# Fetching the token-major x one granule earlier, its squares ahead of the fifth granule's cast, and 1/rms and one normalisation one granule up

## The chip, the cores and the metric

The kernel runs on one NeuronCore of one Trainium2 chip. The metric is the device time of one execution in microseconds, the median of the runs; lower is better. All inputs are in HBM as fp32 when the time starts, and the fp32 result lies in HBM when it ends. The core has a matrix engine (TensorE, PE in the rows; its weight loads are PEld), a vector engine (VectorE, DVE), a scalar engine (ScalarE, ACT), GpSimd (POOL) and a queue that only issues transfers (SyncE, SP).

## The reference, cut to what matters

One decoder layer on 256 tokens of width 2048. An RMS norm, one wide input projection in nine parts, block attention and a gated spatial unit side by side, two projections merged by sigmoid gates, an output projection and the residual:

```
h = rms_norm(x, norm_g)                 # x * rsqrt(mean(x*x) + 1e-6) * g, per token
q, k, v, z_a, u_b, v_b, z_b, g_a, g_b = split(h @ w_in)
q, k = rms_norm per head
y_a = (attention(q, k, v) * silu(z_a)) @ w_proj_a
y_b = (gelu(u_b) * (W_s norm(gelu(v_b)) + b) * silu(z_b)) @ w_proj_b
out = x + (sigmoid(g_a) * y_a + sigmoid(g_b) * y_b) @ w_out
```

The change concerns the first line alone: when the sum of squares of each token is formed, and when the factor 1/rms made from it is applied to x.

## The kernel before, in words

**Granules.** All weights come in one stream of granules of 1 MB, 128 partitions x 2048 fp32. `schedule()` (L47) lists them: eight for q (numbers 0 to 7), eight for k, then v, z_a, v_b, u_b, z_b, the gates, the two projections and the output. Granule i is loaded by `load` into a tile `raw`, of which there are four, so that granule 4 waits for the release of granule 0's, and so on; from granule 10 on the tiles `t` of the Strassen granules share these four buffers.

**Split fp32.** Every fp32 operand is made into a high part and a low part. `halve` (L119) casts `raw` to `wh` on ScalarE (L120) and subtracts on VectorE to get `wl` (L121). A product then takes three matmuls: low x by `wh`, high x by `wh`, high x by `wl` (`three`, L274). A granule of q is eight such products into four accumulators, 24 matmuls of 128x512.

**q without 1/rms.** q is computed from x times the gain alone (`split_x`, L191: two gain multiplications on ScalarE at L195, the cast `xuh` at L198, the subtraction `xul` on VectorE at L199, for two of the sixteen row tiles of x at a time). The factor 1/rms is a number for each token and is put on when q leaves PSUM (L629). From k on the projections use a normalised x, which must therefore be ready before granule 8.

**The factor 1/rms.** x by tokens, two tiles `xnat` of 128 tokens x 2048 (1 MB each), is loaded at L180. `stats` squares each tile on ScalarE with a running sum (L233) and then calls `rsqrt`: one VectorE instruction (L228) and one power on GpSimd (L229) give `rstd`. `stats_row` (L236) has TensorE transpose `rstd` into a row, broadcast over the partitions (`ps_R`, L239), and ScalarE copies it to SBUF (L240). `normalise(i)` (L245) multiplies half i of x by that row on VectorE (L247). `halves_x` casts and subtracts (`xh`, `xl`, L252 and L253), `forms` and `halves_f` make the sums of x for Strassen's products (`F`, `Fh`, `Fl`).

**Order.** One loop over the granules (L601) issues, at granule i: the load of granule i+3, the split of granule i+2, for i below 4 the split of x for granule i+4, the matmuls of granule i, and then what was registered for i by `at` (L530). So the squares, registered in the kernel before at granule 2, stand on ScalarE's queue behind the cast of granule 4. For ScalarE and VectorE the order of the code is kept up to the end of granule 7 (the block opened at L588 and closed at L603). The order on TensorE and SyncE, and on all engines from granule 8 on, is made by the framework's planner from its own estimates: it can let later work go ahead of an instruction that it believes not yet ready. Each engine carries out its queue strictly in the order that was made.

**The first loads**, on SyncE's queue in the order of L165 to L180: pieces of granule 0 and 1 and of x by features, granule 2, x tiles 8 to 11, granule 3, x tiles 12 to 15, the two `xnat` tiles. Granules 4, 5, ... follow from the loop.

Of the kernel before, what the change touches and what calls it, by code (L numbers as in the profile page):

```python
# [20 lines left out]
P = 128  # L21
S = 256
# [42 lines left out]
def hybrid_layer_kernel(  # L65
# [9 lines left out]
    nc = tc.nc  # L75
# [10 lines left out]
    def slot(dtype, name):  # L86
        return big.tile([P, WORDS], dtype, tag="big", name=name)
# [17 lines left out]
    def load_piece(i, a, b):  # L105
        nc.sync.dma_start(raw[i][:, a:b], w[i, :, a:b])

    def new_raw(i):
        raw[i] = wpool.tile([P, WORDS], F32, tag="raw", bufs=4, name=f"raw{i}")

    def load(i, pieces=1):
        if i >= NG:
            return
        new_raw(i)
        n = WORDS // pieces
        for a in range(pieces):
            load_piece(i, a * n, (a + 1) * n)
# [43 lines left out]
    def load_x(p0, p1):  # L161
        nc.sync.dma_start(xt[p0 // 8][:, p0 % 8:(p1 - 1) % 8 + 1, :],
                          xT[:, NVEC + p0 * S:NVEC + p1 * S].rearrange("p (k t) -> p k t", t=S))
# [9 lines left out]
    load_x(4, 8)  # L173
    load(2, pieces=2)
    load_x(8, 12)
    load(3)
    load_x(12, 16)
    xn = [slot(F32, f"xnat{m}") for m in range(2)]
    for m in range(2):
        nc.sync.dma_start(xn[m], x[m * P:(m + 1) * P, :])  # L180
    for i in range(2):
        xu_h.append(slot(F32R, f"xuh{i}").rearrange("p (k t) -> p k t", t=S))
        xu_l.append(slot(F32R, f"xul{i}").rearrange("p (k t) -> p k t", t=S))
# [346 lines left out]
    def at(i, fn, *a):  # L530
        later.setdefault(i, []).append((fn, a))
# [5 lines left out]
        fn(*a, free["banks"][n0:n1])  # L537

    i0 = first["q", 0]
    at(i0 + 2, stats)  # L540
    at(i0 + 3, stats_row)
    at(i0 + 4, normalise, 1)
    at(i0 + 4, halves_x, 1)
    at(i0 + 5, normalise, 0)
    at(i0 + 5, forms)
# [2 lines left out]
    i0 = first["k", 0]  # L548
    at(i0 + 1, sums, None, "q")
    at(i0 + 3, norm_qk, "q")  # L550
    i0 = first["v", 0]
# [3 lines left out]
    i0 = first["za", 0]  # L555
# [4 lines left out]
    i0 = first["vb", 0]  # L560
# [6 lines left out]
    i0 = first["ub", 0]  # L567
# [4 lines left out]
    i0 = first["zb", 0]  # L572
# [3 lines left out]
    i0 = first["g", 0]  # L576
# [148 lines left out]
```

## Time and profile before

| | |
|---|---|
| median of 3 runs | 687.62 us (687.28 to 688.37) |
| the profiled execution's own time | 687.05 us |
| its span, first to last instruction | 685.3 us |
| busy share of the span: TensorE, VectorE, ScalarE, GpSimd | 97%, 81%, 57%, 5% |
| granted TensorE clock, mean | 0.995 of full speed |
| HBM read, written | 132.72 MB, 2.10 MB |

The span runs from the first to the last instruction; 1.75 us of the execution's time lie outside it. A row of the timeline gives the start in microseconds, the duration, the engine (SPq is SyncE's queue), the source line, the operation, out<-in, shapes and how many were merged (x2), and in brackets how long the engine was idle before it and what released it. A granted clock of 1.00 is TensorE's higher level, 2.4 GHz, and 0.50 the lower, 1.2 GHz.

### The profile page before, as it was taken

How to read it: one execution, taken by the hardware profiler on the slowest of the kernel's cores; microseconds unless marked ns; L12 is line 12 of the kernel's file. 1: busy time of each engine (PE TensorE's matmuls, PEld its weight loads, DVE VectorE, ACT ScalarE, POOL GpSimd, SP SyncE). 2: the span in 40 equal slices, each digit the busy share in tenths (PEclk: the TensorE clock that was granted, in tenths of full speed). 3: DMA queues.
4: the chain of work that ended last, by engine and by line, in shares of the span. 5: the costliest groups of instructions: out<-in, count | busy, mean ns of one | idle time of the engine just before them, and what ended most of it. 6: DMA issues, size and time to landing. Idle time of an engine off the chain costs nothing.

```text
span 685.3 us, 7695 instructions
## 1 busy us (share of the span) xinstructions
PE 664.1 (97%) x3018; PEld 545.4 (80%) x3018; DVE 554.3 (81%) x504; ACT 390.4 (57%) x459; POOL 31.9 (5%) x28
## 2 busy tenths in 40 slices
PE   8789999999999999999989999999999999999997
PEld 5578778778888887788777888888888888888886
DVE  4569989889899899998998998878869886754551
ACT  7678757765775585665745735663554555333330
POOL 1000401200000007000000000000000000000000
PEclk9989999999999999999999999999999999999999
DMA  8952653483373535634735824844664466857610
GB/s 312 418 193 67 241 213 117 166 303 124 119 280 129 229 134 184 245 103 153 297 125 223 304 85 185 315 175 184 230 239 143 188 258 225 261 184 233 235 46 31
DMA packets 21923, 135.31 MB, mean 197 GB/s; under 512 B 2432, under 2 KB 3072, under 8 KB 6656
## 3 DMA queue, kind: packets, MB, share of 16 engines
q1 hardware_dynamic: 20736, 132.73, 52.4%
q10 hardware_dynamic: 1152, 2.10, 1.2%
q8 instruction: 23, 0.38, 0.2%
q14 instruction: 12, 0.10, 0.0%
HBM read 132.72 MB, written 2.10 MB: 197 GB/s over the span
## 4 chain that ended last, share of the span: by engine, by line
PE 69%; DVE 15%; issue 5%; ACT 4%; DMA 4%; SPq 1%; POOL 0%; DVEq 0%; ACTq 0%
PE acc_g L279 14%; PE y L279 13%; PE acc_out L279 13%; PE seven_g L279 5%; PE acc_za L279 4%; PE acc_vb L279 4%; DMA raw<-in_w 4%; DVE wl L121 3%; ACT th L120 2%; PE acc_zb L279 2%; DVE wlp L121 2%; PE acc_v L279 2%; DVE t L138 2%; DVE tl L121 2%; PE acc_ub L279 2%
## 5 line engine op out<-in xcount | busy, mean ns | idle before, releaser
L121 DVE TENSOR_TENSOR wl<-raw,wh 128x2048 fp32r<-128x2048 f32 (+2 forms) x87 | 183.2, 2116 | 68.0 <-ACT wh L120 67.8
L120 ACT CAST wh<-raw 128x2048 fp32r<-128x2048 f32 (+2 forms) x87 | 153.7, 1774 | 103.8 <-PE acc_out L279 45.7
L120 ACT CAST th<-t 128x2048 fp32r<-128x2048 f32 x40 | 76.4, 1911 | 106.9 <-DVE t L141 102.2
L121 DVE TENSOR_TENSOR tl<-t,th 128x2048 fp32r<-128x2048 f32 x40 | 91.6, 2291 | 29.1 <-ACT th L120 28.6
L279 PE MATMUL acc_out<-wh,mT 128*128 128x512 f32 x256 | 79.0, 390 | 0.0
L120 ACT CAST whp<-raw 128x1536 fp32r<-128x1536 f32 x40 | 59.2, 1482 | 29.9 <-DMA raw<-in_w 18.9
L121 DVE TENSOR_TENSOR wlp<-raw,whp 128x1536 fp32r<-128x1536 f32 x40 | 70.5, 1763 | 0.0
L279 PEld LDWEIGHTS acc_out<-wh,mT 128*128 128x128 f32 x256 | 47.9, 188 | 9.8
L279 PE MATMUL acc_out<-wl,mT 128*128 128x512 f32 x128 | 49.8, 389 | 0.0
L279 PE MATMUL acc_g<-wh,xh 128*128 128x512 f32 x128 | 49.8, 389 | 0.0
L279 PE MATMUL acc_g<-wh,xl 128*128 128x512 f32 x128 | 49.7, 389 | 0.0
L138 DVE TENSOR_TENSOR t<-raw 128x1024 f32<-128x1024 f32 x40 | 49.2, 1230 | 0.5
L279 PE MATMUL acc_g<-wl,xh 128*128 128x512 f32 x128 | 48.8, 389 | 0.0
L229 POOL TENSOR_TENSOR rs<-ms,mhalf 128x4 f32<-128x4 f32 x12 | 25.2, 2119 | 128.4 <-DVE ms L228 128.4
L279 PEld LDWEIGHTS acc_g<-wl,xh 128*128 128x128 f32 x128 | 24.0, 188 | 5.1
L279 PEld LDWEIGHTS acc_g<-wh,xl 128*128 128x128 f32 x128 | 24.0, 188 | 5.1
L279 PEld LDWEIGHTS acc_out<-wl,mT 128*128 128x128 f32 x128 | 24.0, 188 | 5.0
L279 PEld LDWEIGHTS acc_g<-wh,xh 128*128 128x128 f32 x128 | 24.0, 188 | 4.9
L140 DVE TENSOR_TENSOR t<-t,raw 128x512 f32<-128x512 f32 x40 | 27.5, 689 | 0.3
L141 DVE TENSOR_TENSOR t<-t,raw 128x512 f32<-128x512 f32 x40 | 27.5, 688 | 0.3
L279 PE MATMUL acc_q<-wh,xuh 128*128 128x512 f32 x64 | 25.5, 399 | 1.6 <-ACT wh L120 1.6
L279 PE MATMUL acc_q<-wl,xuh 128*128 128x512 f32 x64 | 25.7, 401 | 0.3 <-DVE wl L121 0.2
(453 smaller groups left out, 1427.8 us busy)
## 6 DMA issues: line engine op xcount, KB each, us to landing
raw<-in_w SPq DMA_DIRECT2D x117, 1024.0 KB, 4.9
raw<-in_w SPq DMA_DIRECT2D x5, 512.0 KB, 7.3
xnat<-in_x SPq DMA_DIRECT2D x2, 1024.0 KB, 13.3
xres<-in_x ACTq DMA_DIRECT2D x8, 256.0 KB, 5.8
out<-xres SPq DMA_DIRECT2D x7, 256.0 KB, 4.7
xt<-in_xT SPq DMA_DIRECT2D x3, 512.0 KB, 9.9
raw<-in_w SPq DMA_DIRECT2D x2, 256.0 KB, 4.6
ws<-in_wsT SPq DMA_DIRECT2D x2, 256.0 KB, 2.9
```

Source lines behind the costliest of these rows:

```text
L120: nc.scalar.copy(h, r)
L121: nc.vector.tensor_tensor(l, r, f(h), op=ALU.subtract)
L138: nc.vector.tensor_tensor(two, r[:, B:3 * B].rearrange("p (a n) -> p a n", a=2), r[:, None, 0:B].to_broadcast([P, 2, B]), op=ALU.add)
L140: nc.vector.tensor_tensor(t[:, 2 * B:3 * B], t[:, 0:B], r[:, 2 * B:3 * B], op=ALU.add)
L141: nc.vector.tensor_tensor(t[:, 3 * B:], t[:, 2 * B:3 * B], r[:, 3 * B:], op=ALU.add)
L229: nc.gpsimd.tensor_tensor(dst, ms[:, :n], mhalf[:, :n], op=ALU.pow)
L279: nc.tensor.matmul(acc, a, b, start=(start and n == 0), stop=(stop and n == 2))
```

## The change

The loads of the two `xnat` tiles move from behind x tiles 12 to 15 to around the load of granule 3: the first ahead of it, the second behind it, and x tiles 12 to 15 come ahead of both. Three registrations change: `stats` from granule 2 to granule 1, so that the squares stand in front of the cast of granule 4 on ScalarE's queue; `normalise(1)` from granule 4 to granule 3, so that it stands in front of granule 6's subtraction on VectorE's queue. `stats_row` stays at granule 3, `halves_x(1)` at granule 4. (The diff's first registration line moves `stats`; 1/rms is formed inside it.) No instruction is added or left out.

```
     load(2, pieces=2)
     load_x(8, 12)
-    load(3)
     load_x(12, 16)
     xn = [slot(F32, f"xnat{m}") for m in range(2)]
-    for m in range(2):
-        nc.sync.dma_start(xn[m], x[m * P:(m + 1) * P, :])
+    nc.sync.dma_start(xn[0], x[0:P, :])
+    load(3)
+    nc.sync.dma_start(xn[1], x[P:S, :])
...
     i0 = first["q", 0]
-    at(i0 + 2, stats)
+    at(i0 + 1, stats)
     at(i0 + 3, stats_row)
-    at(i0 + 4, normalise, 1)
+    at(i0 + 3, normalise, 1)
     at(i0 + 4, halves_x, 1)
```

## Rows read from the trace of the kernel before

**Rows 1.** Busy time in stretches of the span. The columns: the stretch in us from the span's start and its length; busy us of TensorE, its weight loads, VectorE, ScalarE and GpSimd, each with its number of instructions; the granted TensorE clock, the busy share of the DMA engines, GB/s.

```profile
29.80:36.50 6.70, 0.00 (x0) 0.00 (x0) 3.06 (x3) 6.67 (x9) 0.69 (x1) 0.72 1.01 415
36.50:40.00 3.50, 3.43 (x10) 2.83 (x11) 2.66 (x2) 3.47 (x6) 0.02 (x1) 0.56 0.21 89
...
250.00:685.30 435.30, 426.48 (x1922) 351.88 (x1919) 341.24 (x298) 216.35 (x196) 13.92 (x4) 1.00 0.52 191
```

**Rows 2.** TensorE's timeline: the start of granule 3, its last matmul, the transposes of 1/rms, granule 4's first matmuls, and the start of granule 8 (the first of k).

```profile
24.15 0.39 PE L279 MATMUL acc_q<-wh,xul 128*128 128x512 f32 x1
...
29.36 0.39 PE L279 MATMUL acc_q<-wl,xuh 128*128 128x512 f32 x1
36.57 0.69 PE L239 MATMUL ps_R<-ident,rstd 128*128 128x128 f32 x2 [6.82 <-POOL rstd L229]
36.91 0.78 PE L279 MATMUL acc_q<-wh,xul 128*128 128x512 f32 x1
...
39.19 0.58 PE L279 MATMUL acc_q<-wl,xuh 128*128 128x512 f32 x1
39.60 0.40 PE L279 MATMUL acc_q<-wh,xul 128*128 128x512 f32 x1
...
60.04 0.39 PE L279 MATMUL acc_k<-wh,xl 128*128 128x512 f32 x1
```

**Rows 3.** ScalarE's timeline from the cast of granule 3 to that of granule 6 and `xh`.

```profile
19.41 1.91 ACT L120 CAST wh<-raw 128x2048 fp32r<-128x2048 f32 x1
...
28.36 1.91 ACT L120 CAST wh<-raw 128x2048 fp32r<-128x2048 f32 x1 [5.58 <-DMA raw<-in_w]
30.17 0.91 ACT L195 ACTIVATE xt<-xt,xv 128x256 f32<-128x256 f32 x2
...
31.63 1.91 ACT L233 ACTIVATE xnat<-xnat 128x2048 f32<-128x2048 f32 x1
...
35.43 1.88 ACT L120 CAST wh<-raw 128x2048 fp32r<-128x2048 f32 x1
...
38.67 0.37 ACT L240 COPY xv<-ps_R 128x256 f32<-128x256 f32 x1
38.94 1.91 ACT L120 CAST wh<-raw 128x2048 fp32r<-128x2048 f32 x1
45.41 1.91 ACT L252 CAST xh<-xt 128x2048 fp32r<-128x2048 f32 x1 [4.56 <-DVE xt L247]
```

**Rows 4.** VectorE's timeline from granule 3's subtraction to the second normalisation, and granule 8's subtraction; then GpSimd's row for the power.

```profile
21.36 2.29 DVE L121 TENSOR_TENSOR wl<-raw,wh 128x2048 fp32r<-128x2048 f32 x1 [1.17 <-ACT wh L120]
...
30.30 2.29 DVE L121 TENSOR_TENSOR wl<-raw,wh 128x2048 fp32r<-128x2048 f32 x1 [6.05 <-ACT wh L120]
...
37.34 2.29 DVE L121 TENSOR_TENSOR wl<-raw,wh 128x2048 fp32r<-128x2048 f32 x1 [1.62 <-ACT wh L120]
...
40.88 2.29 DVE L121 TENSOR_TENSOR wl<-raw,wh 128x2048 fp32r<-128x2048 f32 x1 [0.65 <-ACT wh L120]
43.09 2.29 DVE L247 TENSOR_TENSOR xt<-xt,xv 128x2048 f32<-128x2048 f32 x1
47.35 2.29 DVE L253 TENSOR_TENSOR xl<-xt,xh 128x2048 fp32r<-128x2048 f32 x1 [1.98 <-ACT xh L252]
...
51.77 2.28 DVE L247 TENSOR_TENSOR xt<-xt,xv 128x2048 f32<-128x2048 f32 x1
...
58.17 2.28 DVE L121 TENSOR_TENSOR wl<-raw,wh 128x2048 fp32r<-128x2048 f32 x1
...
35.81 0.71 POOL L229 TENSOR_TENSOR rstd<-ms,mhalf 128x2 f32<-128x2 f32 x1 [32.71 <-DVE ms L228]
```

**Rows 5.** Transfers: SyncE's issues (start, duration) of granule 3, x tiles 12 to 15 and granule 4, and, from the view of the transfers issued in that moment, KB and us from issue to landing of granule 3, x tiles 12 to 15 and granule 4; last the lines of the view of `xnat` with the issues of its two tiles and their times to landing.

```profile
8.48 0.33 SPq L106 DMA_DIRECT2D raw<-in_w  x1
9.16 0.33 SPq L162 DMA_DIRECT2D xt<-in_xT  x1
14.34 0.33 SPq L106 DMA_DIRECT2D raw<-in_w  x1
raw<-in_w SPq DMA_DIRECT2D x1, 1024.0 KB, 10.8
xt<-in_xT SPq DMA_DIRECT2D x1, 512.0 KB, 11.4
raw<-in_w SPq DMA_DIRECT2D x1, 1024.0 KB, 13.9
L180 SPq DMA_DIRECT2D xnat<-in_x x2: 328/328/328, 10.4 to 11.7; - x2
...
DMA to landing us min/median/max: 12.6/13.3/13.9
```

**Rows 6.** TensorE's first wait that the timeline names after granule 4, the matmul behind it, and the cast on ScalarE that it waited for; then TensorE's longest wait from 60 us on; last, from the view of waits from 60 us on (us in total, times, longest), the group with the largest total.

```profile
94.07 0.50 PE L279 MATMUL acc_k<-th,xl 128*128 128x512 f32 x1 [0.75 <-ACT th L120]
94.41 0.40 PE L279 MATMUL acc_k<-th,xh 128*128 128x512 f32 x1
...
92.11 1.91 ACT L120 CAST th<-t 128x2048 fp32r<-128x2048 f32 x1 [4.41 <-DVE t L141]
...
354.07 0.50 PE L279 MATMUL acc_g<-th,xl 128*128 128x512 f32 x1 [1.72 <-ACT th L120]
...
PE acc_g L279 <- ACT th L120: 3.1, 2, 1.7
```

## The prediction, written before the result was known

> **What bounds the kernel now.** I read first the busy shares, then the windows, then TensorE's timeline where a window shows it idle, and from there the queues that feed it. TensorE is busy 97% of the span, so time can be won only where it stands still. From 250 us on it lacks 8.8 us of 435 (435.30 - 426.48, [rows 1]); the largest hole by far is one, at 29.8 to 36.5 us, with no matmul at all, and behind it the granted clock is 0.56 for 3.5 us [rows 1].
>
> The hole is read in three steps. TensorE ends granule 3 with the matmul of 29.36 and next in its queue stand the transposes of 1/rms (`ps_R`), which wait 6.82 us for GpSimd's `rstd` [rows 2]. `rstd` ends at 36.5 (35.81 + 0.71, [rows 4]) because ScalarE starts the squares only at 31.63. And the squares start there because ahead of them on ScalarE stands the cast of granule 4, which idled 5.58 us for its transfer [rows 3]: that landed at 28.24 (issue 14.34 + 13.9), while the second `xnat` had been there since 25.6 (11.7 + 13.9, [rows 5]). So ScalarE waits for granule 4 with work in hand. The DMA engines are saturated all the while (share 1.01, 415 GB/s, [rows 1]), so landings are a matter of order.
>
> After the hole the first matmuls run at the lower clock: from 36.91 to 39.60 there are six, 2.69 us instead of 6 x 0.2265 = 1.36 (the pace of granule 3: 23 steps from 24.15 to 29.36, [rows 2]). Price of one cold start: 1.33 us. The seventh matmul of granule 4 starts at 39.60; that is my mark.
>
> **The change, part by part.**
>
> *The loads.* Granule 3 now goes behind x tiles 12 to 15 (0.5 MB) and one `xnat` (1 MB). Before it landed at 19.28 (8.48 + 10.8), the x tiles at 20.56 (9.16 + 11.4), 1.28 later, the first `xnat` at 23.0 (10.4 + 12.6), 2.44 later [rows 5]. So granule 3 lands some 3.8 us later, at 23.1. All the same bytes stand ahead of the second `xnat` and of granule 4, which land as before, at 25.6 and 28.24. SyncE's queue has the same number of entries, and no entry of it gets a wait that it had not.
>
> The Trainium skill ("DMA: Bandwidth & Descriptors", section "Where 436 GB/s comes from") holds that for transfers from HBM the HBM side, some 358 GB/s for a core, is what limits; an estimate from that gives 1.57 MB / 358 GB/s = 4.4 us for the delay, and a sum smaller by 0.6 us. The rows show 415 GB/s here and do not agree with it, and I go by the rows.
>
> *ScalarE.* Idle gaps do not count in what follows; I take the distances from start to start that the queue shows when it runs without waiting [rows 3]: cast of a granule to the gain multiplications 1.81 (28.36 to 30.17), from there to the next entry 1.46 (to 31.63), squares to the next cast 3.80 (31.63 to 35.43), cast to the copy of the row 3.24 (35.43 to 38.67), copy to the next cast 0.27. New: cast 3 at 23.2 (it was 19.41), squares at 23.2 + 3.27 = 26.5, both `xnat` being there, cast 4 at 30.3 (28.36 before, so 1.9 us later; its data lie ready for 2 us, this is what the move costs), cast 5 at 33.5 (35.43), the copy of the row at 36.8 (38.67), cast 6 at 37.05 (38.94).
>
> *1/rms.* Squares to the end of the power is 36.52 - 31.63 = 4.89 us before, so `rstd` is there at 31.4 instead of 36.5.
>
> *VectorE.* From a cast's start to its subtraction 1.94, the subtraction 2.29 (28.36, 30.30, [rows 3, 4]). Granule 3's low part is ready at 23.2 + 1.94 + 2.29 = 27.4, granule 4's at 34.5 (32.6 before), granule 5's at 37.7. Then `normalise(1)` starts at 38.3 (behind an `xul` of 0.7; the row is ready at 37.2) instead of 43.09, granule 6's subtraction at 40.5 instead of 40.88, `xh` at 40.6 instead of 45.41. From here each step is 2.2 us, start to start (40.88 to 43.09), and none waits: `xl` 42.7, granule 7 at 44.9, `normalise(0)` 47.1 instead of 51.77. The idle 1.98 us before `xl` [rows 4] goes, since granule 6's subtraction now covers the cast. VectorE's chain gains 4.7 us.
>
> *TensorE.* Granule 3 could start at 24.15 [rows 2] but its high part is ready at 25.1 and its low part at 27.4. With the order of matmuls of granule 4 (low x, high x, then `wl`) the third starts at 27.5, the rest follow in 0.34 (the first step after a wait, 94.07 to 94.41, [rows 6]) + 21 x 0.2265, so granule 3 ends near 32.6, 3 us later than before. This loss is hidden: granule 4's low part comes at 34.5 only. The transposes take 0.34 (36.57 to 36.91, [rows 2]) from 32.6, `rstd` having been ready for over 1 us; two matmuls follow, and the third of granule 4 starts at 34.55, the seventh at 34.55 + 0.34 + 3 x 0.2265 = 35.6. Against 39.60 that is **4.0 us won**. The slack of the cover is 34.55 - (32.6 + 0.34 + 0.45) = 1.15 us; each us that granule 3 lands later than 23.1 costs a full us, through ScalarE's queue as well.
>
> *Is it kept?* Granules 5, 6 and 7 would start at 39.6, 45.1 and 50.5; their low parts are ready at 37.7, 42.8 and 47.2. Granule 8 would start at 56.0 (60.04 - 4.0) and its low part (start 58.17 before, 53.5 after) is ready at 55.8. The next wait named is at 94.07, 0.75 us for a cast at the end of VectorE's chain [rows 6]. If that chain keeps its 4.7 us, the wait shrinks by 0.6 and the gain grows to 4.6; if the planner, which orders both engines from granule 8 on, uses it otherwise, it stays 4.0, or less. I take the middle, **4.3 us**. The profiled execution (687.05, 1.75 of it outside the span) is 0.57 below the median of 687.62; the gain is in the span and carries to the median: 687.62 - 4.3 = **683.3 us**.
>
> *Unknowns.* Whether the clock falls in the new hole: from 24.4 to 27.5 TensorE has only two matmuls. Above, a pause of 6.82 us ended at the lower level [rows 1, 2]; one of 1.72 us did not ([rows 6]; clock 1.00 from 250 us on, [rows 1]). This lies between, nearer to the second, so I take no fall; a fall costs 0 (inside granule 3, under the 1.15 us of slack) to 1.33. And the planner's order on TensorE: if granule 4's matmuls with `wh` are put ahead of those with `wl`, TensorE starts at 32.9 without the wait for `wl` and the seventh comes at 34.4, 5.2 won, the upper end; VectorE's chain caps it near 4.7 at 94 us. If it wins nothing, the lower end is below.
>
> **Rivals.**
>
> *A. Granule 3 too late or TensorE cold (gain 1.4 to 2.9).* If the clock falls before granule 4 the gain is 4.0 - 1.33 = 2.7, 684.9 us; a landing of granule 3 at 24.5 gives the same. For it: the 3.1 us with little work. Against: each pause is short, and the rate of 415 GB/s is steady.
>
> *B. The transposes ahead of granule 3 on TensorE.* The change would not do what it says: the planner, believing 1/rms early, could queue `ps_R` in front of granule 3's matmuls. TensorE then stands from 24.4 to 31.4, as long as before, goes cold, and granule 4's seventh matmul comes at 31.4 + 0.34 + 24 x 0.2265 + 1.33 + 6 x 0.2265 = 39.9. Gain -0.3 there, up to +0.6 later by the smaller wait at 94 us: 687.0 to 687.9 us, no change. Against: before, the transposes stood behind all of granule 3.
>
> *C. Slower: the planner's new order behind granule 7.* The places of the `th` casts and of the additions before them, on ScalarE and VectorE from granule 8 on, come from estimates, and the start that they are made from moves. One cast placed too late cost 1.72 us, and the gates lost 3.1 us in two of them [rows 6]. If four more casts fall like that, 4 x 1.72 = 6.9 us are lost against 4.3 won: 690.2 us. It decides from 4.3 us of new waits, and is over the bound for slower from 5.7. For: nothing fixes that order. Against: all that those engines wait for comes earlier by about the same amount, and all waits of TensorE behind 250 us are only 8.8 us [rows 1].
>
> **How the numbers follow.** Forecast 72% (682.3 to 684.6 by itself), A 13%, B 8%, C 7%. 0.2%, 1.4 us, is about what a measurement of this kernel tells from no change. Faster: the forecast and nearly all of A, 0.83; the same: B and the tail of A, 0.10; slower: C, 0.07. The range goes from 5.6 won (the upper end of 5.2 and 0.4 of run-to-run spread) to 1.4 won: 682.0 to 686.2.
>
> **What would show it.** In the profile after: granule 3's cast near 23.2 and the squares at 26.5, ahead of a cast of granule 4 at 30.3; `rstd` at 31.4; no TensorE pause over 2.5 us, two short ones before the low parts of granules 3 and 4; granule 8 starting near 56.0; `normalise(0)` at 47.1. Granule 3 landing after 24.5, a clock under 1 between 25 and 37 us, or `ps_R` ahead of granule 3 would prove the steps wrong; a granule 8 at 56 with a time over 685 would prove the carrying wrong.

## The result, and the profile after

The changed kernel takes 681.98 us (median of 4 runs, 681.6 to 682.29) against 687.73 for the kernel before, run beside it: a ratio of 0.9915, 95% interval 0.9898 to 0.9933. That is 5.75 us less; the forecast was 4.3 us less, with the low end of its range at 682.0, so the measured time lies just below the range. The profiled execution has a span of 679.8 us, 5.5 less than before.

The start first. TensorE's timeline of the changed kernel: granule 3's first three matmuls, the transposes of 1/rms, granule 4's third, fourth and seventh matmul, and granule 8's first.

```profile
25.19 0.50 PE L279 MATMUL acc_q<-wh,xul 128*128 128x512 f32 x1 [0.80 <-ACT wh L120]
25.53 0.40 PE L279 MATMUL acc_q<-wh,xuh 128*128 128x512 f32 x1
27.52 0.50 PE L279 MATMUL acc_q<-wl,xuh 128*128 128x512 f32 x1 [1.59 <-DVE wl L121]
...
32.64 0.38 PE L239 MATMUL ps_R<-ident,rstd 128*128 128x128 f32 x2
...
34.58 0.50 PE L279 MATMUL acc_q<-wl,xuh 128*128 128x512 f32 x1 [1.08 <-DVE wl L121]
34.92 0.40 PE L279 MATMUL acc_q<-wh,xul 128*128 128x512 f32 x1
...
35.62 0.40 PE L279 MATMUL acc_q<-wh,xul 128*128 128x512 f32 x1
...
56.06 0.39 PE L279 MATMUL acc_k<-wh,xl 128*128 128x512 f32 x1
```

Where `ps_R` had a bracket of 6.82 us [rows 2] it has none: 1/rms was there first. The brackets now name the two low parts, the seventh matmul comes at 35.62 instead of 39.60, and granule 8 at 56.06 instead of 60.04. ScalarE's, VectorE's and GpSimd's timelines show what stands behind this, to be held against [rows 3] and [rows 4]: the cast of granule 3, the first square, the cast of granule 4, the copy of the row and `xh`; the subtraction of granule 4, `normalise(1)`, granule 6's subtraction and `normalise(0)`; the power.

```profile
23.23 1.91 ACT L120 CAST wh<-raw 128x2048 fp32r<-128x2048 f32 x1 [3.68 <-DMA raw<-in_w]
...
26.50 1.91 ACT L233 ACTIVATE xnat<-xnat 128x2048 f32<-128x2048 f32 x1
...
30.30 1.90 ACT L120 CAST wh<-raw 128x2048 fp32r<-128x2048 f32 x1
...
36.83 0.37 ACT L240 COPY xv<-ps_R 128x256 f32<-128x256 f32 x1
...
40.81 1.92 ACT L252 CAST xh<-xt 128x2048 fp32r<-128x2048 f32 x1 [1.81 <-DVE xt L247]
```

```profile
32.23 2.29 DVE L121 TENSOR_TENSOR wl<-raw,wh 128x2048 fp32r<-128x2048 f32 x1 [1.63 <-ACT wh L120]
...
38.49 2.29 DVE L247 TENSOR_TENSOR xt<-xt,xv 128x2048 f32<-128x2048 f32 x1
40.70 2.28 DVE L121 TENSOR_TENSOR wl<-raw,wh 128x2048 fp32r<-128x2048 f32 x1
...
47.30 2.29 DVE L247 TENSOR_TENSOR xt<-xt,xv 128x2048 f32<-128x2048 f32 x1
...
30.68 0.71 POOL L229 TENSOR_TENSOR rstd<-ms,mhalf 128x2 f32<-128x2 f32 x1 [27.58 <-DVE ms L228]
```

The cast of granule 4 has no bracket any more: it starts when the squares let it, 30.30, not when its data land. So the start gave 4.0 us. The other 1.5 us of the span came later. I take the first matmul of each part in TensorE's timeline and subtract it from the same matmul's start before:

| first matmul of | k | v | z_a | v_b | u_b | z_b | gates | last of all |
|---|---|---|---|---|---|---|---|---|
| earlier than before by, us | 3.98 | 3.25 | 4.44 | 4.08 | 4.15 | 5.83 | 5.68 | 5.52 |

k gives 0.7 back, v wins 1.2, z_a gives 0.4 back, and one stretch, from u_b's first matmul to z_b's, wins 1.7. TensorE's waits from 36 us on in the kernel after (first block) and from 40 us on in the one before (second block; total, times, longest) show where: those in u_b are gone. (The gates lose about the same in both, 3.2 and 3.1 us.)

```profile
PE acc_g L279 <- ACT th L120: 3.2, 2, 1.8
PE acc_v L279 <- DVE tl L121: 0.9, 1, 0.9
PE acc_k L279 <- ACT th L120: 0.6, 1, 0.6
PE acc_k L279 <- DVE wl L121: 0.5, 1, 0.5
PE acc_zb L279 <- ACT th L120: 0.5, 1, 0.5
```

```profile
PE acc_g L279 <- ACT th L120: 3.1, 2, 1.7
PE acc_v L279 <- ACT th L120: 1.3, 2, 0.7
PE acc_ub L279 <- ACT th L120: 0.8, 1, 0.8
PE acc_k L279 <- ACT th L120: 0.8, 1, 0.8
PE acc_ub L279 <- DVE tl L121: 0.7, 1, 0.7
...
PE acc_v L279 <- DVE tl L121: 0.2, 1, 0.2
```

What differs in u_b is an order. VectorE's timeline before (first block) and after (second), from the second addition `t` of a Strassen granule (L140) to its low part `tl`, which TensorE waits for:

```profile
257.66 0.69 DVE L140 TENSOR_TENSOR t<-t,raw 128x512 f32<-128x512 f32 x1
258.26 1.76 DVE L121 TENSOR_TENSOR wlp<-raw,whp 128x1536 fp32r<-128x1536 f32 x1
259.94 0.69 DVE L141 TENSOR_TENSOR t<-t,raw 128x512 f32<-128x512 f32 x1
260.54 0.38 DVE L228 TENSOR_SCALAR ms<-ss 128x4 f32<-128x4 f32 x4
261.90 1.93 DVE L365 SCALAR_TENSOR_TENSOR vb_c<-vb_c,rs,gain 128x128 f32<-128x128 f32 x7 [0.98 <-POOL rs L229]
263.74 2.28 DVE L121 TENSOR_TENSOR tl<-t,th 128x2048 fp32r<-128x2048 f32 x1
```

```profile
254.26 0.68 DVE L140 TENSOR_TENSOR t<-t,raw 128x512 f32<-128x512 f32 x1
254.87 0.43 DVE L228 TENSOR_SCALAR ms<-ss 128x4 f32<-128x4 f32 x2
255.20 0.69 DVE L141 TENSOR_TENSOR t<-t,raw 128x512 f32<-128x512 f32 x1
255.84 2.19 DVE L365 SCALAR_TENSOR_TENSOR vb_c<-vb_c,rs,gain 128x128 f32<-128x128 f32 x8
257.95 2.28 DVE L121 TENSOR_TENSOR tl<-t,th 128x2048 fp32r<-128x2048 f32 x1
```

Two things have moved. Before, a subtraction of 1.76 us, `wlp`, stands between the two additions; after, it has gone ahead of them. And before, the small `ms` instructions (L228) stand behind the additions, so that VectorE then waits 0.98 us for the powers that GpSimd makes from them (`rs`); after, they stand further ahead and this wait is gone. Counted from u_b's first matmul (244.63 and 240.48) the second of the two additions starts 15.3 us in before and 14.7 after, and `tl` 19.1 and 17.5, 1.6 earlier. VectorE keeps this lead up to the second wait: the cast `th` that TensorE waits for at 281.04 in the kernel before starts 34.45 us in (279.08), in the kernel after 32.82 (273.30). The planner, which makes this order, gives exactly two orders from v on in the kernels that follow, one as before (A) and one as after (B); I read it from the order in which the instructions of each built kernel stand, compared part by part from v to z_b; the order in which TensorE, VectorE and ScalarE carried them out in the traces is the same.

### The profile page after: what moved, and what is told of

It is laid out like the page before. It is cut to its first block, busy times and chain, and to the rows that moved or that the text cites. A ratio compares the mean times of both kernels' runs of the same rounds, so it can differ in the third digit from the quotient of the medians.

```text
span 679.8 us, 7696 instructions
## 1 busy us (share of the span) xinstructions
PE 663.5 (98%) x3018; PEld 544.1 (80%) x3018; DVE 554.6 (82%) x504; ACT 390.7 (57%) x459; POOL 33.3 (5%) x28
## 4 chain that ended last, share of the span: by engine, by line
PE 73%; DVE 12%; issue 4%; DMA 4%; ACT 4%; POOL 0%; SPq 0%; DVEq 0%; ACTq 0%
PE acc_g L279 14%; PE y L279 13%; PE acc_out L279 13%; PE seven_g L279 5%; PE acc_ub L279 4%; PE acc_za L279 4%; DMA raw<-in_w 4%; PE acc_vb L279 4%; DVE wl L121 3%; PE acc_v L279 2%; PE acc_zb L279 2%; DVE wlp L121 2%; ACT th L120 2%; DVE tl L121 2%; PE seven_za L279 2%
## 5 line engine op out<-in xcount | busy, mean ns | idle before, releaser
L140 DVE TENSOR_TENSOR t<-t,raw 128x512 f32<-128x512 f32 x40 | 27.7, 693 | 0.3
```

What stands on the lines that cost most here:

```text
L140: nc.vector.tensor_tensor(t[:, 2 * B:3 * B], t[:, 0:B], r[:, 2 * B:3 * B], op=ALU.add)
```

## The experiments

The change has three parts: the loads, the squares (1/rms is formed inside the same `stats`, so that only two registrations move, not three as "The change" has it) and `normalise(1)`. Two theories were put against each other. **Theory 1, the order:** what was won beyond the start comes from order B. **Theory 2, the lead:** it comes from VectorE being earlier, whatever the order. The loads and the squares alone leave order A; `normalise(1)` at granule 3 gives B, unless `forms` moves too.

**`normalise(1)` alone.**

```
-    at(i0 + 4, normalise, 1)
+    at(i0 + 3, normalise, 1)
```

> Loads and squares as before; only normalise(1) goes one granule up, which by itself gives the planner's new order behind granule 7. Theory 1, the order: granule 4's seventh matmul stays at 39.6, and some 1.5 us are won all the same, most of it between the first and the last matmul of u_b (44.6 us before, 42.9 after the full change): 686.2 us. Theory 2, the lead: what was won beyond the start came from VectorE being earlier, not from the order; u_b stays at 44.6 us and the time at 687.7.

Measured: 685.56 us, ratio 0.997 (0.9959 to 0.998). The start is as before: the transposes wait 6.80 us and q ends 0.6 us later than before in the two traces (0.4 of that is there when the transposes start, 36.95 against 36.57). u_b's first and last matmul:

```profile
243.79 0.39 PE L279 MATMUL acc_ub<-wh,xl 128*128 128x512 f32 x1
...
286.75 0.39 PE L279 MATMUL acc_ub<-wl,xh 128*128 128x512 f32 x1
```

42.96 us, as in the changed kernel (42.90), against 44.57 before. v, to z_a's first matmul, takes 43.89 against 45.26. This fits theory 1, with some 2 us for order B without any gain at the start, rather more than the 1.5 expected. It does not yet exclude theory 2, since VectorE is a little earlier here too (granule 8's subtraction at 57.26 against 58.17).

**All but `normalise(1)`**, the loads and the squares moved (the edit against the changed kernel):

```
     at(i0 + 3, stats_row)
-    at(i0 + 3, normalise, 1)
+    at(i0 + 4, normalise, 1)
```

> The full change without the move of normalise(1), so with the planner's old order behind granule 7. Theory 1, the order: granule 4's seventh matmul at 35.6, u_b takes 44.6 us as before, and of the 4.0 us won at the start up to 2 are lost at granule 8, because VectorE's chain is only 1.9 us earlier there: 683.7 to 685.7 us. Theory 2, the lead: u_b 1.7 us shorter than before, 682 to 684 us.

Measured: 685.26 us, ratio 0.9965 (0.9951 to 0.9978). u_b takes 44.51 us:

```profile
243.28 0.39 PE L279 MATMUL acc_ub<-wh,xl 128*128 128x512 f32 x1
...
287.79 0.39 PE L279 MATMUL acc_ub<-wl,xh 128*128 128x512 f32 x1
```

So a kernel that starts earlier, but has order A, wins nothing in u_b. Its q ends only 3.1 us earlier. The transfers were issued later in this trace (granule 3's at 11.45 us against 10.49 in the full change), so that granule 4's low part is ready at 35.4 instead of 34.5; this accounts for the 0.9 us that are missing. The clock fell in granule 3 as well (below), but that was hidden behind the same low part. k gives 2.2 back: TensorE waits 0.68, 0.85 and 0.67 us, for a low part and two `th`, where it waited once before, 0.75 us.

**Squares and `normalise(1)`, loads as before**, run twice:

```
-    at(i0 + 2, stats)
+    at(i0 + 1, stats)
...
-    at(i0 + 4, normalise, 1)
+    at(i0 + 3, normalise, 1)
```

> Squares and normalise(1) moved, loads as before. Granule 3 then lands at 19.3 and its cast isn't late; the squares start at 23.0, when the first token tile lands, the cast of granule 4 at 28.4, its low part is ready at 32.6 and granule 4's seventh matmul comes at 33.7: 5.9 us won at the start, 1.9 more than with the moved loads. Theory 1, the order: 5.9 + 1.5, 680.3 us. Theory 2, the lead: the same or a little better, 679.5 to 680.5. If the moved loads were what let the squares go first, the start wins less than 4.0: over 682.

> Squares and normalise(1) moved, loads as before, once more, beside the full change on the same chip. If the moved loads cost 1.9 us at granule 4 (seventh matmul at 35.6 against 33.7), this is 1.8 us faster than the full change: 680.2 against 682.0. If the first run of it was luck, the two are equal.

Measured: 680.17 us, ratio 0.9898 (0.9884 to 0.9911), and, on the same chip as a second run of the full change, 680.96, ratio 0.9902 (0.9888 to 0.9915). u_b: 42.88 and 42.93. The 680.3 expected was met the first time; the profiled executions, however, won only 3.3 and 3.9 us at the start, not 5.9. ScalarE's timeline of the first of them, and TensorE's low part of granule 4:

```profile
25.25 1.92 ACT L233 ACTIVATE xnat<-xnat 128x2048 f32<-128x2048 f32 x1 [0.49 <-DMA xnat<-in_x]
...
29.37 1.90 ACT L120 CAST wh<-raw 128x2048 fp32r<-128x2048 f32 x1 [2.11 <-DMA raw<-in_w]
...
33.64 0.72 PE L279 MATMUL acc_q<-wl,xuh 128*128 128x512 f32 x1 [1.59 <-DVE wl L121]
34.16 0.63 PE L279 MATMUL acc_q<-wh,xul 128*128 128x512 f32 x1
```

Granule 4 landed 15.3 us after its issue, not 13.9 [rows 5], and behind the wait the matmuls run 0.43 apart, at the lower clock. In the second run it landed after 15.4 us and the clock did not fall. With the squares alone, where the loads are the same, it landed after 13.9; why it was later here is not shown. These profiled executions were the slowest of either series (681.73 and 682.15), so what the faster ones did at the start is not shown either. Without the moved loads the kernel is 0.8 to 1.8 us faster than with them by the medians; the intervals of the two ratios overlap, so that it beats the full change is likely and not settled.

**The squares alone:**

```
-    at(i0 + 2, stats)
+    at(i0 + 1, stats)
```

> Only the squares move; loads and normalise(1) as before, so the planner's old order. Seventh matmul of granule 4 at 33.7. Theory 1, the order: u_b 44.6 us as before; 5.9 us won less up to 2 at granule 8, where VectorE's chain is late: 681.8 to 683.8 us. Theory 2, the lead: u_b 1.7 us shorter as well: 680.2 to 682.2.

Measured: 683.83 us, ratio 0.9948 (0.9936 to 0.9961). Here the low part of granule 4 came where it was expected (third matmul at 32.47) and q ends 6.1 us earlier than before. u_b takes 44.48 us, and k gives back 2.25 of the 6.1: with `normalise(1)` behind granule 6, VectorE is late there, as in the run of all but `normalise(1)`. VectorE is 3.95 us earlier than before at granule 8's subtraction (54.22 against 58.17), and u_b wins nothing from it: this speaks against theory 2.

**The full change again.**

> The full change once more, on the same chip as the three runs beside it. Both theories: 682.0 us; u_b 42.9 us from its first to its last matmul. The clock at the wait for granule 4's low part (34.6 us) may or may not fall this time: it fell after a wait of 1.59 us in two of the kernels run so far and not after the 1.59 us of the first run of this one.

Measured: 681.75 us, ratio 0.9914 (0.9901 to 0.9927); u_b 42.88; the clock did not fall.

**The full change, but `forms` one granule later** (the edit against the changed kernel).

```
-    at(i0 + 5, forms)
+    at(i0 + 6, forms)
```

> The full change, with `forms` one granule later. normalise(1) stays early on VectorE, but the planner's order from v on is then exactly the old one, while k gets an order of its own. Theory 1, the order: u_b 44.6 us as before the change, 1.7 longer than with the change, and the time some 1.7 us above it, plus or minus what k's order does: 683.0 to 685.0. Theory 2, the lead of VectorE through the early normalise(1): u_b 42.9 us as with the change, 682.0.

This separates order B from an early `normalise(1)`, which the four kernels of the first set cannot do. Measured: 684.9 us, ratio 0.9959 (0.9947 to 0.9971). u_b's first and last matmul, and TensorE's waits there:

```profile
242.78 0.39 PE L279 MATMUL acc_ub<-wh,xl 128*128 128x512 f32 x1
...
287.32 0.39 PE L279 MATMUL acc_ub<-wl,xh 128*128 128x512 f32 x1
```

```profile
PE acc_ub L279 <- ACT th L120: 0.8, 1, 0.8
PE acc_ub L279 <- DVE tl L121: 0.7, 1, 0.7
```

44.54 us: the waits of the kernel before are back, to the tenth. v wins nothing either (45.32 us to z_a against 45.26). The time is 3.1 us above the full change on the same chip, at the far end of what was expected. In the two traces v, z_a and u_b together are 2.5 us longer, q ends 1.8 later (0.4 of it because the transfers came later, the rest at the lower clock, below), and k is 0.4 shorter.

**The loads alone.**

```
     load_x(8, 12)
-    load(3)
     load_x(12, 16)
     xn = [slot(F32, f"xnat{m}") for m in range(2)]
-    for m in range(2):
-        nc.sync.dma_start(xn[m], x[m * P:(m + 1) * P, :])
+    nc.sync.dma_start(xn[0], x[0:P, :])
+    load(3)
+    nc.sync.dma_start(xn[1], x[P:S, :])
```

> The moved loads alone. Granule 3's cast comes at 23.2 and granule 3 ends at 32.6, but the squares still stand behind granule 4's cast (28.4), so 1/rms comes at 36.5 as before and the late granule 3 is hidden: 687.6, or 686.3 if the shorter pause (4.0 us instead of 6.8) leaves the clock high. If a late granule 3 costs by itself: up to 690.6.

Measured: 687.51 us, ratio 1.0 (0.9992 to 1.0009). Granule 3 is late and hidden, as said: it waits for its cast and its low part, and the transposes come 0.2 us after their place before (36.57).

```profile
27.26 0.79 PE L279 MATMUL acc_q<-wl,xuh 128*128 128x512 f32 x1 [1.59 <-DVE wl L121]
...
36.74 0.43 PE L239 MATMUL ps_R<-ident,rstd 128*128 128x128 f32 x2 [2.80 <-POOL rstd L229]
```

All ten traces side by side; the gain at the start is how much earlier than before q's last matmul starts, and u_b is from its first to its last matmul:

| kernel | `normalise(1)` | order from v on | gain at the start | u_b |
|---|---|---|---|---|
| before | late | A | 0 | 44.57 |
| loads alone | late | A | -0.4 | 44.54 |
| all but `normalise(1)` | late | A | 3.1 | 44.51 |
| squares alone | late | A | 6.1 | 44.48 |
| full, `forms` later | early | A | 2.2 | 44.54 |
| `normalise(1)` alone | early | B | -0.6 | 42.96 |
| full change, twice | early | B | 4.0, 4.0 | 42.90, 42.88 |
| loads as before, twice | early | B | 3.3, 3.9 | 42.88, 42.93 |

u_b goes with the order and with nothing else that was changed: neither 6 us at the start nor an early `normalise(1)` moves it. So does z_a's loss (48.0 to 48.1 us to v_b's first matmul with A, 48.4 with B). v is less clear: to z_a's first matmul it takes 44.7 to 45.3 us with A and 43.9 to 44.5 with B.

## Why the prediction was right or wrong, point by point

*What bounds the start*: right. The wait for `rstd` went, and the low parts of granules 3 and 4 took its place.

*The loads, ScalarE, 1/rms, VectorE, TensorE*: right to 0.2 us. Cast of granule 3 at 23.23 (23.2 forecast), squares 26.50 (26.5), cast of granule 4 30.30 (30.3), the power's end 31.39 (31.4), `normalise(1)` 38.49 (38.3), `normalise(0)` 47.30 (47.1), granule 4's seventh matmul 35.62 (35.6), granule 8 at 56.06 (56.0). The term of 4.0 us stands. That a late granule 3 is hidden was seen in the loads alone too, there behind a wait for 1/rms that still lasted 2.80 us.

*The figure of the Trainium skill for the loads* ("DMA: Bandwidth & Descriptors", section "Where 436 GB/s comes from"): by its 358 GB/s the cast of granule 3 would have come at 23.8. It came at 23.23, where the 415 GB/s of the rows put it, so the trace does not agree with it.

*Is it kept?*: wrong, and this is the step that failed. I carried the 4.0 us to 94 us along the old order, let VectorE's chain add up to 0.6 there (0.3 in the sum), and put what the planner makes of the rest at nothing in the sum, a risk alone. In fact k gave 0.7 back, at two new waits, granule 9's low part and a `th` (0.54 and 0.57 us), in place of the one of 0.75; behind k, under order B, 2.5 were won: 1.2 in v, -0.4 in z_a and 1.7 in u_b; what follows gave 0.2 back. Together 5.5 in the span, 5.75 in the medians, instead of 4.3. The 1.7 and the -0.4 are shown to be the order's; of the 1.2 in v an unknown part is, since three kernels with order A were 0.3 to 0.6 us shorter there than the kernel before.

k's loss can be read from the traces. All kernels with order B have one and the same order on TensorE in k as well. In it the first matmul with granule 9's low part has its place 5.9 us behind k's first matmul; in the kernel before, 8.4. VectorE's order there has not changed. These are its subtractions for granule 9 before, in the full change and with `normalise(1)` alone:

```profile
64.77 2.29 DVE L121 TENSOR_TENSOR wl<-raw,wh 128x2048 fp32r<-128x2048 f32 x1
...
60.32 2.28 DVE L121 TENSOR_TENSOR wl<-raw,wh 128x2048 fp32r<-128x2048 f32 x1
...
63.87 2.28 DVE L121 TENSOR_TENSOR wl<-raw,wh 128x2048 fp32r<-128x2048 f32 x1
```

They end 7.0, 6.5 and 5.5 us behind k's first matmul (60.04, 56.06, 60.63). So the full change waits; `normalise(1)` alone has the same order, does not wait there, and its k is 0.3 us shorter than before. The new order costs k time only because TensorE won nearly as much at the start (4.0) as VectorE's chain (4.5).

The upper end of the range, which the measured time all but met, was worked out from something else: matmuls of granule 4 with `wh` going ahead of those with `wl`. Those kept their order (third matmul at 34.58, behind its wait), so that the time came out so near it is luck.

*Rival C*, the planner's new order, had the mechanism, and for the sum of it the wrong sign. It said only that the start from which the planner works moves, not which part of the change moves it. The runs show it: the loads and the squares leave the order behind granule 7 untouched; the place of `normalise(1)` alone turned A into B.

*Rival A*, the cold clock, did not come in the two profiled executions of the change, but did in other kernels with the same pause; in one of them it cost more than I bounded (below). *Rival B* did not come: the transposes stayed behind granule 3.

What stays open: how much of v's 1.2 us is the order's; whether, and by how much, the kernel without the moved loads is faster; and why granule 4 landed late in both its profiles.

## What to carry to other kernels

When a planner orders part of a kernel, a change has two prices: that of the moved work, which rows gave to 0.2 us in the full change, though they missed by 2 us and more where a transfer landed later (squares and `normalise(1)` with the loads as before); and that of the order that comes out, which has either sign. Before trusting an attribution, list the order of every part behind the change, and look for an edit that moves the work and keeps the order, or the other way round. A stage's own length, first to last matmul, told the two apart here to a tenth of a microsecond, where the whole times spread by 1 to 2 us.

## What was not expected of the hardware

The granted clock of 24 to 36 us differed between kernels with the same pauses ahead of granule 3's high and low part, of 0.5 to 1.0 and 1.59 us with two matmuls between. In the changed kernel it stayed at 1.00, in both its profiles; with all but `normalise(1)` it was 0.86, with `forms` later 0.72, with the loads alone 0.86. The windows of 24 to 36 us of the full change, of all but `normalise(1)`, and of `forms` later (columns as in [rows 1]):

```profile
24.00:36.00 12.00, 8.52 (x36) 6.08 (x35) 6.47 (x6) 11.94 (x15) 0.71 (x1) 1.00 1.00 388
```

```profile
24.00:36.00 12.00, 9.65 (x36) 7.10 (x36) 5.92 (x5) 11.78 (x13) 0.71 (x1) 0.86 0.91 375
```

```profile
24.00:36.00 12.00, 9.41 (x30) 6.85 (x28) 6.05 (x6) 11.94 (x14) 0.71 (x1) 0.72 0.91 371
```

One and the same kernel does both: with the loads as before the clock fell behind pauses of 1.18 and 1.59 us in the first run, and stayed at 1.00 behind longer ones, 1.78 and 1.59, in the second. So the length of these pauses alone does not decide it; what does, these runs do not show.

The transposes came at 34.89 and 35.83 in the two kernels with a fall, instead of 32.64, later by 2.3 and 3.2 us. I had bounded such a fall at 1.33 us, the price of one cold start in [rows 2], with 1.15 of slack against it. With all but `normalise(1)` this held: six matmuls ran at the lower clock, which cost 1.4 us, and granule 4's third matmul came 0.15 us behind its low part (35.58 and 35.43). With `forms` later it did not: 13 matmuls ran at the lower clock, which cost 2.8 us, and granule 4's third matmul came 1.6 us behind its low part (36.51 and 34.92).
